# Raw tiles of p_v from four to eight, the order of products at the layer joints, and gates applied as scalars in a decoder trunk

## The chip, the cores and the metric

The kernel runs on one core of a Trainium2 chip, as one program. The metric is the device time of one execution in microseconds. Of the core's engines the text names TensorE (PE, with its weight loads as PEld), VectorE (DVE), ScalarE (ACT), GpSimd (POOL) and SyncE (SP), whose instruction stream here only issues DMA transfers.

## What is computed

Two layers over 256 positions of width 1024. Layer 0 is latent attention (MLA) and a PEER feed-forward layer, layer 1 is native sparse attention (NSA) and a second PEER. Each sub-layer ends in a normalization.

```python
x = layer_norm(ALPHA * x + f(x))          # after every sub-layer

def peer_ffn(x, w_q, subkeys, u, v):      # 16384 experts, 8 heads x 16 per token
    q = (xc @ w_q).reshape(PEER_CHUNK, PEER_HEADS, 2, PEER_DK // 2)
    ...                                   # top 16 x 16 of two key halves, best 16
    u_e = u[experts]
    v_e = v[experts]
    a = gelu(einsum("thkd,td->thk", u_e, xc))
    return einsum("thk,thkd->td", g * a, v_e)

def masked_softmax(sc, mask):             # NSA: one for each branch and head
    sc = jnp.where(mask, sc, NEG_INF)
    m = jnp.max(sc, axis=-1, keepdims=True)
    e = jnp.exp(sc - m) * mask
    return e / jnp.maximum(jnp.sum(e, axis=-1, keepdims=True), TINY)
...                                       # o = sum over 3 branches of gate[branch, head] * p @ v
```

## The kernel before

**Weights in two parts.** Every weight matrix is read from HBM as float32 tiles of 128x1024 (512 KB). A tile lands in a raw buffer. ScalarE casts it to a high part `hi` (L98), VectorE subtracts that from the raw tile and gets the low part `lo` (L109). Activations are split likewise, so a product needs up to three matmuls: high by high, high by low, low by high. All 603 tiles stand in one list, `self.stream`, in the order of use. `_sdma` requests them through SP's queue, `_shi` casts, `_slo` subtracts, and `nxt` hands out the next tile. There are four raw buffers. When `_slo` has recorded the subtraction of a tile, its raw buffer is free, and `_slo` requests the tile three places after the next one to be subtracted (`self.sl + self.nraw - 1`).

**Four parts of the program.** MLA lasts to about 124 us, then the first PEER, NSA, and the second PEER. A PEER layer reads 16 tiles of `p_wq` to route, then 128 tiles of `p_u` (the u phase, in which all activations of all experts are computed and those not chosen are masked), then 128 tiles of `p_v` (the v phase). A stretch between two parts, with sum, normalization, transposition and the first products of the next part, is called a joint here: joint 1 from MLA to the first PEER (about 113 to 132 us), joint 2 from there to NSA (868 to 890), joint 3 from NSA to the second PEER (1040 to 1061), and the end.

**The v phase.** For each tile j of `p_v` TensorE does ten matmuls of 128x512 (L160, in `v_mm`): six for the first 128 tokens (`tt` 0) and four for the second 128 (`tt` 1). Their other operand, `W`, is the masked activations of these 128 experts, split into parts on ScalarE (L740) and VectorE (L745). Of the second 128 tokens only 64 go through these matmuls, with high and low part of W side by side as 128 columns; so the result has the low part's product in its rows 64 to 127, and `sum_1` adds both halves (L812 to L814). The other 64 tokens have 128 experts each, and their rows of `p_v` are gathered: 64 indirect DMAs from GpSimd's queue (L447, `g_row`), 512 KB each, into a ring of ten buffers `row` and `more`. VectorE multiplies each row by its factor and adds it up (L461, `g_mac`, into `gacc`), from tile 7 on, one row per 1.77 tiles. Before that small gathers (L451, `g_act`) fetch the activations for the factors. After the last row `g_sum` (L805, L806) adds `gacc` to the residual `hN`. The kept tiles, the last eight, have their matmuls for `tt` 1 done in the joint, so that TensorE has work while the first half is normalized.

**The joint.** `ln_sum`, `ln_stats`, `ln_mid` and `ln_scale` normalize halves of 512 columns (L232, L235, L239 to L251, L257) on VectorE. `ln_aside` does one half of `tt` 0 on ScalarE (L266) and GpSimd (L267, L268). `ln_T` transposes on TensorE (L189) and splits into high part (L282, ScalarE) and low part (L283, VectorE) of the transposed activations `hT`. Low parts of the next weight tiles are made on GpSimd in that time (`self._slo(..., nc.gpsimd)`). `early_open` starts the next part's products with two tiles for `tt` 0, all three kinds, and `early_close` does the rest tile by tile.

**NSA.** Per pair of heads the scores come from TensorE, VectorE takes maxima and reciprocals and multiplies the probabilities `p` by them and by the gates (L1505 to L1526); for heads 8 to 13 a part of that runs on GpSimd. GpSimd also subtracts for the low part of q (L1323, `qs`) and zeroes three buffers (`hb`, `kcp` at L1375, `hidR` at L1384).

**What sets the order.** Instructions run on each engine in the order in which the code records them; a queue of DMA requests goes in order too. Most of the order is written out by hand, with deferred steps (`tick`, `run_side`) between them.

Of the kernel before, what the change touches and what calls it, by code (L numbers as in the profile page):

```python
# [37 lines left out]
RING, MORE, LEAD = 6, 4, 7  # L38
# [4 lines left out]
class Kern:  # L43
# [5 lines left out]
    def plan(self):  # L49
        I, L = self.I, []  # L50
        if "mla" in self.parts:
            L += [I["a_w_in"][k] for k in range(KC)]
            L += [I["a_wk"][i] for i in range(2)]
            L += [I["a_wq"][i] for i in range(3)]
            L += [I["a_wv"][i] for i in range(2)]
            L += [I["a_wq"][i] for i in range(3, 6)]
            L += [I["a_wo"][i] for i in range(KC)]
        for l in (0, 1):
# [8 lines left out]
            if f"peer{l}" in self.parts:  # L67
                L += [I["p_wq"][l, i] for i in range(16)]
                L += [I["p_u"][l, (P - FIRST + j) % P] for j in range(P)]
                L += [I["p_v"][l, j] for j in range(P)]  # L70
        self.stream = L
        self.si = 0
# [28 lines left out]
    def _slo(self, upto, eng=None):  # L101
        while self.sl <= min(upto, len(self.stream) - 1):
# [8 lines left out]
            self._sdma(self.sl + self.nraw - 1)  # L111
# [27 lines left out]
    def new_hT(self):  # L139

        self.hTT = self.pers.tile([P, KC, 2, S], F32R, tag="hT", name="hT")
# [119 lines left out]
    def ln_aside(self, tt, hf):  # L261

        nc, w = self.nc, self.lnw[tt]
        z, gb, acc = self.ln_half(tt, hf)
        nc.vector.scalar_tensor_tensor(w[:, 0:1], w[:, 2:3], -1.0, w[:, 7:8], op0=OP.mult, op1=OP.mult)
        nc.scalar.activation(z, z, AF.Identity, bias=w[:, 0:1], scale=w[:, 7:8])  # L266
        nc.gpsimd.tensor_tensor(z, z, gb[:, 0, :], op=OP.mult)  # L267
        nc.gpsimd.tensor_tensor(z, z, gb[:, 1, :], op=OP.add)  # L268
        if not self.want_T:
            nc.sync.dma_start(self.O[0, tt * P:(tt + 1) * P, hf * 512:(hf + 1) * 512], z)  # L270

# [13 lines left out]
    def ln_first(self):  # L285

        for hf in range(2):
            self.ln_sum(0, hf)
            self.ln_stats(0, hf)
        self.ln_mid(0)  # L290
        for hf in range(2):
            self.ln_scale(0, hf)
        lo = [self.ln_T(0, hf) for hf in range(2)]
        self.ln_sum(1, 0)
        lo[0]()
        self.ln_stats(1, 0)
        self.ln_sum(1, 1)
        lo[1]()
        self.ln_stats(1, 1)

    def ln_last(self, *los):
        los = list(los)
# [110 lines left out]
    def peer(self, l):  # L413
        tc, nc, I = self.tc, self.nc, self.I
        with ExitStack() as es:
# [23 lines left out]
            def g_row(c):  # L439
                if c >= P // 2:  # L440
                    return
                if c % (RING + MORE) >= RING:
                    t = more[:, c % (RING + MORE) - RING]
                else:
                    t = gat.tile([P, D], F32, tag="row", name="row", bufs=RING)
                grow[c] = t
                nc.gpsimd.indirect_dma_start(out=t, out_offset=None, in_=gtable,  # L447
                                             in_offset=bass.IndirectOffsetOnAxis(ap=gidx[:, 0, c:c + 1], axis=0))
# [5 lines left out]
            def g_mac(c):  # L454
# [7 lines left out]
                g_row(c + RING + MORE)  # L462
# [179 lines left out]
            if not hasattr(self, "eacc") or self.parts[0] == f"peer{l}":  # L642
                self._slo(self.si + 1)
# [140 lines left out]
            def v_mm(j, tt, blocks, start=False, stop=False):  # L784
# [8 lines left out]
            more = self.pers.tile([P, MORE, D], F32, tag="hT", name="more")  # L793
            rate, gc = (P - 8 - LEAD) / 64, 0

            fetch = deque([(g_row, c) for c in (RING, RING + 1)] + [(g_act, c) for c in range(4)] +
                          [(g_row, c) for c in (RING + 2, RING + 3)] + [(g_act, c) for c in range(4, 64)])
            summed = []

            def g_sum():  # L800

                t = gat.tile([P, D], F32, tag="row", name="gsum", bufs=RING)
                u, z = slice(P - GT, P), hN[P - GT:P, 1, :]
                nc.scalar.copy(t[u], gacc[0:GT])
                nc.vector.scalar_tensor_tensor(z, z, ALPHA, gacc[u], op0=OP.mult, op1=OP.add)  # L805
                nc.vector.tensor_tensor(z, z, t[u], op=OP.add)  # L806

            def sum_1(f):

                t = gat.tile([P, 512], F32, tag="row", name="low", bufs=RING)  # L810
                c, z = accs[1][f], hN[0:P - GT, 1, f * 512:(f + 1) * 512]
                nc.scalar.copy(t[0:P - GT], c[P - GT:P])  # L812
                nc.vector.scalar_tensor_tensor(z, z, ALPHA, c[0:P - GT], op0=OP.mult, op1=OP.add)
                nc.vector.tensor_tensor(z, z, t[0:P - GT], op=OP.add)  # L814

            for j in range(P):
# [14 lines left out]
                for _ in range(8 if j == 0 else 1):  # L831
                    if fetch:
                        f, c = fetch.popleft()
                        f(c)
# [3 lines left out]
                if gc == 64 and not summed:  # L838
                    summed.append(1)
                    g_sum()  # L840
# [12 lines left out]
            self.ln_scale(0, 0)  # L853
            if early:
                self._slo(self.si, nc.gpsimd)
            self.ln_aside(0, 1)
            for j in range(P - NT, P - 2):
# [776 lines left out]
```

## Time and profile before

| | us |
|---|---|
| median of three runs | 1817.84 (1814.76 to 1824.02) |
| the profiled execution | 1817.85 |
| its span in the trace | 1816.1 |
| VectorE, ScalarE, GpSimd busy | 1558.2, 1047.1, 490.7 |
| DMA over the span | 416.69 MB, 229 GB/s |

The clock that TensorE was granted is 0.987 of full speed over the span. The profile says for each group of instructions how long they ran, how long the engine sat idle before them, and whose event ended that idle time. Matmul ends are modelled; a matmul's start is measured. Distances between starts are therefore what is used for TensorE's pace.

### The profile page before, as it was taken

The numbers are of one execution on the slowest core, as the hardware profiler recorded it, in microseconds if no ns is written. First come the engines' busy times: TensorE is split into PE (matmuls) and PEld (weight loads), VectorE is DVE, ScalarE is ACT, GpSimd is POOL, SyncE is SP. The second block draws the span as 40 slices with busy tenths as digits, with TensorE's granted clock in tenths as the row PEclk, the third lists the DMA queues.
The fourth block names the chain that finished last, engine by engine and source line by source line (L and its number), as shares of the span: only waits on it lengthen the run. The fifth ranks groups of instructions, "written<-read, shape, count | busy, mean of one in ns | idle before, by whom it ended". The sixth has DMA issues, their size and how long they took to land. (4 is left out here: it accounts for less than half of the span.)

```text
span 1816.1 us, 30995 instructions
## 1 busy us (share of the span) xinstructions
PE 1747.9 (96%) x10610; PEld 1500.9 (83%) x10610; DVE 1558.2 (86%) x3692; ACT 1047.1 (58%) x2271; POOL 490.7 (27%) x457
## 2 busy tenths in 40 slices
PE   7989999999999999999898999999999999999996
PEld 6869999888888777887786689998888887778775
DVE  6778988889998889998658779988899986899998
ACT  6645456666666455555457645556666664555553
POOL 2120002000004776540533310011000016775510
PEclk9999999999999999999998999999999999999998
DMA  7545657555557999997661265656555558999983
GB/s 248 161 147 166 194 176 266 178 183 182 176 185 264 350 328 350 352 358 249 241 215 53 94 209 180 193 184 245 189 175 183 185 196 307 335 336 361 344 313 127
DMA packets 120653, 416.69 MB, mean 229 GB/s; under 512 B 18064, under 2 KB 20144, under 8 KB 119408
## 3 DMA queue, kind: packets, MB, share of 16 engines
q1 hardware_dynamic: 91008, 322.61, 53.0%
q0 software_dynamic: 29488, 92.10, 14.0%
q8 instruction: 84, 1.38, 0.3%
q14 instruction: 73, 0.60, 0.1%
HBM read 400.49 MB, written 13.63 MB: 228 GB/s over the span
## 5 line engine op out<-in xcount | busy, mean ns | idle before, releaser
L98 ACT CAST hi<-raw 128x1024 fp32r<-128x1024 f32 (+1 forms) x589 | 616.5, 1048 | 411.6 <-DMA raw<-p_v 140.6
L160 PE MATMUL mm<-hT,hi 128*128 128x256 f32 (+1 forms) x3360 | 845.9, 332 | 0.0
L109 DVE TENSOR_TENSOR lo<-raw,hi 128x1024 fp32r<-128x1024 f32 (+1 forms) x582 | 710.4, 1223 | 99.1 <-ACT hi L98 63.7
L160 PE MATMUL mm<-hT,lo 128*128 128x256 f32 x2376 | 639.7, 281 | 0.0
L160 PEld LDWEIGHTS mm<-hT,hi 128*128 128x128 f32 x3360 | 560.1, 190 | 48.0 <-issue 1.2
L160 PEld LDWEIGHTS mm<-hT,lo 128*128 128x128 f32 x2376 | 451.3, 190 | 13.4
L160 PE MATMUL acc<-hi,W 128*128 128x512 f32 x1476 | 420.9, 392 | 9.0 <-issue 5.0
L160 PEld LDWEIGHTS acc<-hi,W 128*128 128x128 f32 x1476 | 276.8, 188 | 73.5 <-issue 10.6
L160 PE MATMUL acc<-lo,W 128*128 128x512 f32 x984 | 310.7, 396 | 6.7 <-DVE lo L109 3.3
L729 POOL DMA_DIRECT2D actD<-gst x64 | 34.8, 544 | 799.1 <-ACT gst L727 799.1
L160 PEld LDWEIGHTS acc<-lo,W 128*128 128x128 f32 x984 | 181.6, 188 | 61.2 <-DVE lo L109 19.2
L451 POOL DMA_INDIRECT gel<-actD,gidx x128 | 149.7, 1170 | 39.0 <-issue 38.7
L447 POOL DMA_INDIRECT row<-p_v,gidx x80 | 118.1, 1476 | 111.1 <-DVE gacc L461 77.3
L721 ACT ACTIVATE mm<-mm 128x192 f32<-128x192 f32 (+23 forms) x170 | 40.9, 241 | 122.7 <-DVE mm L719 122.7
L745 DVE TENSOR_TENSOR W<-A,W 128x128 fp32r<-128x128 f32 (+1 forms) x512 | 108.1, 254 | 1.8 <-ACT W L740 1.8
L461 DVE SCALAR_TENSOR_TENSOR gacc<-row,gw,gacc 128x1024 f32<-128x1024 f32 x78 | 100.0, 1282 | 0.6
L740 ACT CAST W<-A 128x192 fp32r<-128x192 f32 x256 | 88.1, 346 | 0.0
L622 DVE SCALAR_TENSOR_TENSOR A<-acc,A 128x176 f32<-128x176 f32 (+16 forms) x268 | 56.2, 274 | 36.3 <-PE acc L160 34.0
L719 DVE TENSOR_TENSOR mm<-mm,half 128x256 f32<-128x256 f32 x174 | 74.8, 430 | 12.3 <-ACT half L718 11.7
L447 POOL DMA_INDIRECT more<-p_v,gidx x48 | 69.5, 1448 | 43.7 <-DVE gacc L461 34.3
L724 ACT ACTIVATE A<-mm 128x192 f32<-128x192 f32 (+23 forms) x244 | 67.7, 278 | 8.5 <-DVE lo L109 1.8
L718 ACT COPY half<-mm 128x256 f32<-128x256 f32 x174 | 66.0, 379 | 0.5 <-PE mm L160 0.5
(280 smaller groups left out, 1812.6 us busy)
## 6 DMA issues: line engine op xcount, KB each, us to landing
raw<-p_u SPq DMA_DIRECT2D x256, 512.0 KB
raw<-p_v SPq DMA_DIRECT2D x256, 512.0 KB
raw<-p_wq SPq DMA_DIRECT2D x32, 512.0 KB
actD<-gst POOLq DMA_DIRECT2D x64, 128.0 KB
raw<-b_wo SPq DMA_DIRECT2D x12, 512.0 KB
raw<-a_wo SPq DMA_DIRECT2D x8, 512.0 KB
raw<-s_wT SPq DMA_DIRECT2D x8, 512.0 KB
w<-c_w POOLq DMA_DIRECT2D x4, 1024.0 KB
```

The source lines that it names most:

```text
L98: self.nc.scalar.copy(self.his[i], self.raws[i])
L109: e.tensor_tensor(self.los[i], raw, self.his[i].bitcast(F32), op=OP.subtract)
L160: self.nc.tensor.matmul(out, a, b, start=start, stop=stop)
L447: nc.gpsimd.indirect_dma_start(out=t, out_offset=None, in_=gtable, in_offset=bass.IndirectOffsetOnAxis(ap=gidx[:, 0, c:c + 1], axis=0))
L451: nc.gpsimd.indirect_dma_start(out=gel[c // 4][:, c % 4:c % 4 + 1], out_offset=None, in_=gplaces, in_offset=bass.IndirectOffsetOnAxis(ap=g ...
L461: nc.vector.scalar_tensor_tensor(gacc, t, gw[:, c:c + 1], gacc, op0=OP.mult, op1=OP.add)
L622: nc.vector.scalar_tensor_tensor(y, pv[:, j0:j0 + m], 1.0 / GS, y, op0=OP.mult, op1=OP.mult)
L718: nc.scalar.copy(t, ps[:, S:2 * S])
L719: nc.vector.tensor_tensor(ps[:, 0:S], ps[:, 0:S], t, op=OP.add)
L724: nc.scalar.activation(y[:, n:ND], ps[:, n:ND], AF.Gelu)
L740: nc.scalar.copy(WW[j][:, 0:ND], slot(j))
L745: nc.vector.tensor_tensor(WW[j][:, o:o + c.stop - c.start], slot(j)[:, c], WW[j][:, c].bitcast(F32), op=OP.subtract)
```

## The change

Three groups of edits.

**The v phase.** The gather ring shrinks from ten buffers to six. The buffer of 2 MB that held the other four (`more`, in the place of `hT`, which is not needed during the v phase) becomes four more raw tiles (`spare`). `_ahead` says how far requests may run: in the v phase four tiles further than before, up to the next part's first four; shortly before the v phase not beyond its fourth tile. `g_sum` becomes three steps: `g_alpha` after row 60, `g_copy` after the last row, and a last addition one tile later.

**The joints.** `ln_aside` goes; VectorE normalizes all halves. The high parts of the next four tiles are cast early, and TensorE does all products with high parts (both parts of the activations) before any product with a low part. One low part is made on GpSimd, after a copy of one element that makes it wait for `ln_sum(1, 0)`; the others on VectorE, behind the normalization. The kept tiles are used in another order. `sum_1` reads the copied half from PSUM.

**Sparse attention.** The three buffers are zeroed at its start. q's low part moves to VectorE. The maximum with TINY goes (so the sum of exponentials is divided without that floor), and the gate becomes a second scalar of the multiplication.

```diff
-RING, MORE, LEAD = 6, 4, 7
+RING, LEAD = 6, 7
...
-            t = self.sraw.tile([P, n], F32, tag="raw", name="raw")
+            if self.spare is not None and self.v0 <= self.sd < self.v0 + P and (self.sd - self.v0) % 8 > 3:
+                t = self.spare[:, (self.sd - self.v0) % 8 - 4]
+            else:
+                t = self.sraw.tile([P, n], F32, tag="raw", name="raw")
...
-            self._sdma(self.sl + self.nraw - 1)
+            self._sdma(self._ahead())
+
+    def _ahead(self):
+        n, v0 = self.sl + self.nraw - 1, self.v0
+        if self.spare is not None:
+            n = max(n, min(n + 4, v0 + P + 3))
+        elif v0 - 4 < self.sl < v0 + P:
+            n = min(n, v0 + 3)
+        return n
...
+    def lo_aside(self):
+        t = self.small.tile([P, 1], F32, tag="aside", name="aside")
+        self.nc.gpsimd.tensor_copy(t, self.ln_half(1, 0)[0][:, 0:1])
+        self._slo(self.si, self.nc.gpsimd)
+
+    def ln_last(self, early):
+        los = []
+        if early:
+            self.early_open()
+            self.early_mm(0, 0, 0, (0, 1))
+            self.early_mm(0, 1, 0, (0, 1))
+        los.append(self.ln_T(0, 1))
+        if early:
+            self.early_mm(0, 0, 0, (2, 3))
         for hf in range(2):
             self.ln_scale(1, hf)
             los.append(self.ln_T(1, hf))
+            if early and hf == 0:
+                self.early_mm(1, 0, 0, (0, 1))
...
             def sum_1(f):
-                t = gat.tile([P, 512], F32, tag="row", name="low", bufs=RING)
+                t = self.ps()
                 c, z = accs[1][f], hN[0:P - GT, 1, f * 512:(f + 1) * 512]
+                nc.vector.scalar_tensor_tensor(z, z, ALPHA, c[0:P - GT], op0=OP.mult, op1=OP.add)
                 nc.scalar.copy(t[0:P - GT], c[P - GT:P])
-                nc.vector.scalar_tensor_tensor(z, z, ALPHA, c[0:P - GT], op0=OP.mult, op1=OP.add)
                 nc.vector.tensor_tensor(z, z, t[0:P - GT], op=OP.add)
...
     def early_close(self):
+        for tt in range(2):
+            for x in range(2):
+                self.early_mm(tt, x, 0, range(4))
         for q in range(4):
...
+            self._slo(self.ei + q)
+            if q > 1:
+                self._shi(self.ei + q + 2)
+            self.tick()
+            for tt in range(2):
+                self.early_mm(tt, 0, 1, (q,))
...
-                    nc.gpsimd.tensor_tensor(t[64:128, c], r[:, c], t[0:64, c].bitcast(F32), op=OP.subtract)
+                    nc.vector.tensor_tensor(t[64:128, c], r[:, c], t[0:64, c].bitcast(F32), op=OP.subtract)
...
-                    nc.vector.tensor_scalar(m[:, 2, :], m[:, 2, :], TINY, None, op0=OP.max)
                     nc.vector.reciprocal(m[:, 3, :], m[:, 2, :])
-                    gv = gates[:, :, 16:48].rearrange("p t (b h) -> p t b h", b=2)[:, :, :, h]
-                    nc.vector.tensor_tensor(m[:, 3, :].rearrange("p (t b) -> p t b", t=2),
-                                            m[:, 3, :].rearrange("p (t b) -> p t b", t=2), gv, op=OP.mult)
                     for br, eng in ((1, nc.gpsimd if 8 <= h < NH - 2 else nc.vector), (0, nc.vector)):
-                        eng.tensor_scalar(p[:, br, 0:P], p[:, br, 0:P], m[:, 3, br:br + 1], None, op0=OP.mult)
-                        eng.tensor_scalar(p[:, br, P:384], p[:, br, P:384], m[:, 3, 2 + br:3 + br], None, op0=OP.mult)
+                        for tt, c in enumerate((slice(0, P), slice(P, 384))):
+                            eng.tensor_scalar(p[:, br, c], p[:, br, c], m[:, 3, 2 * tt + br:2 * tt + br + 1],
+                                              gates[:, tt, 16 * br + 16 + h:16 * br + 17 + h], op0=OP.mult, op1=OP.mult)
```

How the order of instructions changes, at three places. Line numbers of the changed kernel are its own: L92 there is the request of a raw tile (L86 before), L181 the matmul (L160), L210 the transposition (L189), L115 the low part (L109).

SP's queue from the last tiles of the first u phase to NSA, before:

```order
L86 DMA raw<-p_wq 128x1024 x16
L86 DMA raw<-p_u 128x1024 x128
L86 DMA raw<-p_v 128x1024 x128
L86 DMA raw<-s_wv 128x1024 x4
L86 DMA raw<-s_wT 128x1024 x4
```

And now, its beginning:

```order
L92 DMA raw<-p_wq 128x1024 x16
L92 DMA raw<-p_u 128x1024 x128
L92 DMA raw<-p_v 128x1024 x4
L92 DMA spare<-p_v 128x1024 x4
L92 DMA raw<-p_v 128x1024 x4
L92 DMA spare<-p_v 128x1024 x4
```

The same 128 transfers stand in the same order; every second four of them go to other buffers, so that a request waits for the tile eight places earlier instead of four.

TensorE in joint 2, from the last products with W (`keep` are the kept tiles; `hi,hT` and `lo,hT` are the first products of NSA, with a weight's high or low part; `ident,hN` are transpositions), before:

```order
L160 MATMUL acc<-lo,W 128x512
L189 MATMUL mm<-ident,hN 128x128 x4
L160 MATMUL acc<-hi,hT 128x512 x8
L160 MATMUL acc<-lo,hT 128x512 x4
L189 MATMUL mm<-ident,hN 128x128 x8
L160 MATMUL acc<-hi,hT 128x512 x4
L160 MATMUL acc<-lo,hT 128x512 x2
L160 MATMUL acc<-hi,hT 128x512 x4
L160 MATMUL acc<-lo,hT 128x512 x2
```

And now:

```order
L181 MATMUL acc<-keep,W 128x512 x16
L210 MATMUL mm<-ident,hN 128x128 x4
L181 MATMUL acc<-keep,W 128x512 x4
L181 MATMUL acc<-hi,hT 128x512 x8
L210 MATMUL mm<-ident,hN 128x128 x4
L181 MATMUL acc<-hi,hT 128x512 x4
L210 MATMUL mm<-ident,hN 128x128 x4
L181 MATMUL acc<-hi,hT 128x512 x4
L210 MATMUL mm<-ident,hN 128x128 x4
L181 MATMUL acc<-hi,hT 128x512 x16
L181 MATMUL acc<-lo,hT 128x512 x16
```

Products with high parts now stand between the transpositions, and all sixteen products with low parts at the end; after the last transposition there are 32 products instead of 36.

VectorE in NSA at the first head's probabilities (`m` holds maxima, sums and reciprocals, `qs` q's parts), before:

```order
L1507 TENSOR_SCALAR m<-m 128x4
L1396 TENSOR_TENSOR vcp<-mm,m_10029 128x512 x2
L1505 TENSOR_REDUCE m<-mm 128x2
L1506 TENSOR_REDUCE m<-acc 128x2
L1507 TENSOR_SCALAR m<-m 128x4
L1519 TENSOR_SCALAR m<-m 128x4
L1520 RECIPROCAL m<-m 128x4
L1522 TENSOR_TENSOR m<-m,gates 128x4
L1525 TENSOR_SCALAR p<-p,m 128x128
```

And now:

```order
L1508 TENSOR_SCALAR m<-m 128x4
L1330 TENSOR_TENSOR qs<-qr,qs 64x512 x2
L1397 TENSOR_TENSOR vcp<-mm,m_9993 128x512 x2
L1506 TENSOR_REDUCE m<-mm 128x2
L1507 TENSOR_REDUCE m<-acc 128x2
L1508 TENSOR_SCALAR m<-m 128x4
L1521 RECIPROCAL m<-m 128x4
L1524 TENSOR_SCALAR p<-p,m,gates 128x128
```

Two small operations are gone from each head's chain, and in four places of VectorE's order two subtractions for q stand ahead of reductions.

More of the change, by code (lines that the diff above doesn't have):

```diff
@@ L110, in _slo, with more_raw @@
             self.sl += 1
-            self._sdma(self.sl + self.nraw - 1)
+            self._sdma(self._ahead())
[6 more added lines that the diff above has]
+        return n
+    def more_raw(self):
+        self.spare = self.pers.tile([P, 4, D], F32, tag="hT", name="spare")
+        self._sdma(self._ahead())
     def nxt(self, prep=True, tick=True):
@@ L439, in g_row @@
             def g_row(c):
[L440 to L448, printed above, removed]
+                if c < P // 2:
+                    t = grow[c] = gat.tile([P, D], F32, tag="row", name="row", bufs=RING)
+                    nc.gpsimd.indirect_dma_start(out=t, out_offset=None, in_=gtable,
+                                                 in_offset=bass.IndirectOffsetOnAxis(ap=gidx[:, 0, c:c + 1], axis=0))
             def g_act(c):
@@ L791, in v_mm, with g_alpha, g_copy @@
                         self.mm(accs[tt][f], xx, ww[:, f * 512:(f + 1) * 512], go, end)
-            more = self.pers.tile([P, MORE, D], F32, tag="hT", name="more")
             rate, gc = (P - 8 - LEAD) / 64, 0
[L796 to L800, printed above, removed]
+            self.more_raw()
+            gu, late_sums = slice(P - GT, P), deque()
+            def g_alpha():
+                nc.vector.scalar_tensor_tensor(gacc[gu], hN[gu, 1, :], ALPHA, gacc[gu], op0=OP.mult, op1=OP.add)
+            def g_copy():
                 t = gat.tile([P, D], F32, tag="row", name="gsum", bufs=RING)
[L803 to L806, printed above, removed]
+                nc.scalar.copy(t[gu], gacc[0:GT])
+                late_sums.append(lambda: nc.vector.tensor_tensor(hN[gu, 1, :], gacc[gu], t[gu], op=OP.add))
             def sum_1(f):
-                t = gat.tile([P, 512], F32, tag="row", name="low", bufs=RING)
+                t = self.ps()
                 c, z = accs[1][f], hN[0:P - GT, 1, f * 512:(f + 1) * 512]
+                nc.vector.scalar_tensor_tensor(z, z, ALPHA, c[0:P - GT], op0=OP.mult, op1=OP.add)
                 nc.scalar.copy(t[0:P - GT], c[P - GT:P])
-                nc.vector.scalar_tensor_tensor(z, z, ALPHA, c[0:P - GT], op0=OP.mult, op1=OP.add)
                 nc.vector.tensor_tensor(z, z, t[0:P - GT], op=OP.add)
@@ L830, in peer @@
                 kept[j] = (hi, lo, WW.pop(j))
[L831 to L834, printed above, removed]
+                for c in range(4) if j == 0 else range(j + 3, min(j + 4, 64)):
+                    g_act(c)
+                if late_sums:
+                    late_sums.popleft()()
                 while gc < 64 and j >= LEAD + int(rate * gc):
@@ L837, in peer @@
                     gc += 1
-                if gc == 64 and not summed:
-                    summed.append(1)
-                    g_sum()
+                    if gc in (60, 64):
+                        late_sums.append((g_alpha, g_copy)[gc == 64])
                 v_mm(j, 0, (0, 1), j == 0, j == P - 1)
@@ L1129, in out_close @@
             self.ln_stats(0, hf)
-        for k in ([5] if again else range(KC - self.kept + 1, 6)):
-            self.out_mm(k, 1, two, False, False)
+        if again:
+            self.out_mm(5, 1, two, False, False)
         if again:
@@ L1260, in nsa @@
             pcT = mp.tile([P, 2, S], F32, name="pcT")
+            hb = tmp.tile([P, 256], F32, tag="hb", name="hb", bufs=1)
+            hr = tmp.tile([P, 2, G, HG, 16], F32, tag="hidR", name="hidR", bufs=1)
+            for x in (hb, kcp, hr):
+                nc.gpsimd.memset(x, 0.0)
             if "peer0" not in self.parts:
-                self._slo(self.si + 1)
+                self._shi(self.si + 3)
                 self.early_open()
```

134 lines of the change are left out of this document (48 added, 86 removed).

## The prediction

> **What bounds the kernel now.** I read the page first, then the table of windows, then waits and single rows.
>
> ```profile
> PE 1747.9 (96%) x10610; PEld 1500.9 (83%) x10610; DVE 1558.2 (86%) x3692; ACT 1047.1 (58%) x2271; POOL 490.7 (27%) x457
> ...
> L109 DVE TENSOR_TENSOR lo<-raw,hi 128x1024 fp32r<-128x1024 f32 (+1 forms) x582 | 710.4, 1223 | 99.1 <-ACT hi L98 63.7
> ```
>
> TensorE is busy for 96% of the span, so nothing here shortens work; only its gaps can go. The windows say where they lie. The columns are the window, its length, then PE, weight loads, DVE, ACT and POOL, the granted clock, the DMA share and GB/s.
>
> ```profile
> 300.00:400.00 100.00, 100.00 (x677) 87.48 (x676) 86.69 (x217) 66.29 (x187) 5.76 (x10) 1.00 0.61 208
> 561.90:870.30 308.40, 300.41 (x1285) 239.22 (x1283) 275.63 (x476) 167.22 (x260) 170.02 (x128) 0.99 0.90 324
> 1489.50:1803.00 313.50, 302.30 (x1280) 238.46 (x1279) 276.08 (x476) 166.13 (x259) 160.79 (x127) 0.99 0.87 311
> 885.00:1042.00 157.00, 144.25 (x1005) 117.73 (x1003) 111.84 (x245) 98.58 (x243) 59.38 (x65) 0.96 0.47 157
> ```
>
> A u phase (first row) has no gap, and the change leaves it alone. The two v phases (rows 2 and 3, from the first product with W to the last) and the sparse attention (row 4) have them. "Busy" hides part of it, because each matmul's modelled duration overlaps the next one's start. The pace shows it better:
>
> ```profile
> 862.76 4.70 PE L160 MATMUL acc<-keep,W 128*128 128x512 f32 x20
> 867.29 0.61 PE L160 MATMUL acc<-hi,W 128*128 128x512 f32 x2
> ```
>
> Twenty products start in 867.29 − 862.76 = 4.53 us, 0.2265 us each. A v phase has 128 tiles × 10 products, 1280 × 0.2265 = 289.9 us. So the phases lose 308.4 − 289.9 = 18.5 and 313.5 − 289.9 = 23.6 us, **42 us** together. What ends the gaps:
>
> ```profile
> ACT hi L98 <- DMA raw<-p_v: 140.6, 109, 5.0
> ```
> ```profile
> 1507.03 0.33 SPq L86 DMA_DIRECT2D raw<-p_v  x1
> ```
> ```profile
> 1523.03 1.04 ACT L98 CAST hi<-raw 128x1024 fp32r<-128x1024 f32 x1 [6.51 <-PE acc L160]
> ```
> ```profile
> 1728.73 6.63 DMA raw<-p_v
> ...
> 1743.15 8.58 DMA raw<-p_v
> ...
> 1786.05 5.16 DMA raw<-p_v
> ```
>
> ScalarE waits 109 times for a raw tile of p_v. One was requested at 1507.03 and only cast at 1523.03, 16 us later; the releaser that this row names had long been done. On the chain of waits single raw transfers take 5.2 to 8.6 us. Four raw tiles at 10 × 0.2265 = 2.27 us of TensorE each give a request at most 9.1 us. So in the v phases late raw tiles are the limit, and not mainly the rate of the DMA:
>
> ```profile
> 700.00:750.00 50.00, 49.63 (x217) 40.04 (x216) 47.94 (x82) 28.85 (x46) 30.06 (x20) 1.00 0.98 357
> ...
> 1700.00:1750.00 50.00, 49.51 (x213) 39.25 (x212) 46.33 (x79) 27.14 (x42) 20.07 (x12) 1.00 0.95 352
> ```
>
> With 357 GB/s moving, 217 products start in 50 us, 0.2304 each, nearly full pace.
>
> **Part A, eight raw tiles in the v phase.** Four rows of the gather ring become four raw tiles: a raw request gets 8 × 2.27 = 18.1 us instead of 9.1, above the 16 us seen. No work is added on an engine, and SP's queue holds the same transfers. What stays of the 42: the DMA rate, and gaps whose releaser is not a raw tile. For the first I take the 0.2304 as pace where rows and raws both flow (113 tiles, since macs start at tile 7 and end at 120): 113 × 10 × 0.0039 = 4.4 us a layer, 9 in all. At the 0.2347 of 1700 to 1750 it would be 9.3 a layer, 19 in all. For the second, 11 us, half of it in the restart of layer 1:
>
> ```profile
> 1519.45 0.39 PE L160 MATMUL acc<-hi,W 128*128 128x512 f32 x1 [1.13 <-DVE gacc L461]
> 1520.87 0.39 PE L160 MATMUL acc<-hi,W 128*128 128x512 f32 x1 [1.03 <-issue]
> ```
>
> Here the next product starts 1.4 us after the one before, and for 1.03 of them TensorE waits for nothing that the trace shows. So 20 of 42 stay, and A gives **−22**; bounds −33 (only 9 stay) and 0 (all of it is rate). VectorE doesn't hinder that: it is busy 275.63 us of the first v phase, over 128 tiles 2.15 us a tile, under TensorE's 2.27, though close. The split g_sum is in the 42: two 64x1024 operations in a row hold up a low part, and TensorE.
>
> ```profile
> 847.98 1.22 DVE L805 SCALAR_TENSOR_TENSOR hN<-hN,gacc 64x1024 f32<-64x1024 f32 x1
> 849.31 1.22 DVE L806 TENSOR_TENSOR hN<-hN,gsum 64x1024 f32<-64x1024 f32 x1
> ```
>
> **Part B, the joints.** A GpSimd operation holds up VectorE. Joint 1:
>
> ```profile
> 116.35 1.82 DVE L239 SCALAR_TENSOR_TENSOR hN<-hN,lnw,gb 128x512 f32<-128x512 f32 x1
> 118.08 0.15 DVE L248 RECIPROCAL lnw<-lnw 128x1 f32<-128x1 f32 x1
> 118.27 2.11 DVE L249 SCALAR_TENSOR_TENSOR lnw<-lnw 128x1 f32<-128x1 f32 x1
> ```
> ```profile
> 115.21 5.16 POOL L109 TENSOR_TENSOR lo<-raw,hi 128x1024 fp32r<-128x1024 f32 x2
> ```
> ```profile
> 120.42 0.73 PE L160 MATMUL acc<-lo,hT 128*128 128x512 f32 x2 [2.02 <-POOL lo L109]
> ```
>
> Joint 2 without a GpSimd operation beside it:
>
> ```profile
> 876.25 0.74 DVE L239 SCALAR_TENSOR_TENSOR hN<-hN,lnw,gb 128x512 f32<-128x512 f32 x1
> 876.90 0.15 DVE L248 RECIPROCAL lnw<-lnw 128x1 f32<-128x1 f32 x1
> 877.10 0.22 DVE L249 SCALAR_TENSOR_TENSOR lnw<-lnw 128x1 f32<-128x1 f32 x1
> ```
>
> And joint 3:
>
> ```profile
> 1045.20 2.11 DVE L249 SCALAR_TENSOR_TENSOR lnw<-lnw 128x1 f32<-128x1 f32 x1
> ```
>
> Joint 1 loses (1.82 − 0.74) + (2.11 − 0.22) = 3.0 us, joint 3 at least 2.11 − 0.22 = 1.9, and TensorE waits with them. After the change one low part of 2.6 us (half of 5.16) runs on GpSimd, released after the first half's sum; it should end about when L239 starts, so I credit 2 us in each. The copy that gates it waits for VectorE's sum; behind it on GpSimd's queue stand only loads for the next stage, which before stood behind two low parts. After the last transposition 32 products are left instead of 36, 4 × 0.227 = 0.9. Joints 1 and 3: −2.9 each. Joint 2 and the end, the sum of the last 64 tokens:
>
> ```profile
> 870.97 0.68 DVE L813 SCALAR_TENSOR_TENSOR hN<-hN,acc 64x512 f32<-64x512 f32 x1 [2.86 <-ACT low L812]
> ```
> ```profile
> 1803.35 0.68 DVE L813 SCALAR_TENSOR_TENSOR hN<-hN,acc 64x512 f32<-64x512 f32 x1 [1.81 <-ACT low L812]
> 1804.06 1.58 DVE L814 TENSOR_TENSOR hN<-hN,low 64x512 f32<-64x512 f32 x1
> ```
>
> The first operation no longer waits for ScalarE's copy (I take 1.5 us of joint 2's 2.86 and 0.7 of the end's 1.81; the rest is the wait for the products that are summed), and L814 returns from 1.58 to 0.68. The copy now goes to PSUM; L813 reads PSUM already and takes the same 0.68 as I expect of L814. Joint 2: −1.5 − 0.9, and about 0.9 from products that need no low part yet, −3.3. The end has no such products: −0.7 − 0.9, so −1.6. The half of the normalization that VectorE takes over (L239 and L257 once more, 0.74 each) lies beside the kept products, 32 × 0.227 = 7.3 us; uncovered it would cost 1.5 in each of four places. Low parts are late next: three of 1.22 on VectorE after the last hT, needed one per 0.9 us (four products), behind sixteen products with high parts; they just fit. B: **−11**, bounds −14 and −4.
>
> **Part C, sparse attention.** Over 16 heads a chain loses two small operations, and GpSimd's subtraction of q moves to VectorE.
>
> ```profile
> L1323 POOL TENSOR_TENSOR qs<-qr,qs 64x512 fp32r<-64x512 f32 x8 | 10.2, 1292 | 11.8 <-issue 8.6 <-ACT qs L1322 3.1
> ```
> ```profile
> L1522 DVE TENSOR_TENSOR m<-m,gates 128x4 f32<-128x4 f32 x16 | 4.4, 274 | 0.6
> ...
> L1519 DVE TENSOR_SCALAR m<-m 128x4 f32<-128x4 f32 x16 | 2.6, 163 | 0.0
> ...
> L1378 DVE TENSOR_TENSOR kcp<-mm,m 128x240 f32<-128x240 f32 x2 | 0.7, 403 | 2.2 <-POOL kcp L1375 2.2
> ```
>
> Removed on VectorE: 4.4 + 2.6 = 7.0 us, and a wait of 2.2 for kcp's zeroing, which now runs long before. Added: eight subtractions of 64x512, about 0.7 each (L813 has that width), 5.6. Only some of the chain shows on TensorE, since the in-order queue now also waits for ScalarE's cast before each subtraction. I take **−3**, bounds −6 and +3.
>
> By the Trainium skill ("SBUF — State Buffer", section "Who interferes with whom") a VectorE operation with two inputs in SBUF blocks against a GpSimd operation that reads SBUF, for its whole length. The joint rows agree: 118.27 + 2.11 = 120.38 is when GpSimd's 115.21 + 5.16 ends. The moved subtraction has two such inputs, so by that rule it can be blocked in its turn; that is the third rival.
>
> **Sum.** −22 − 11 − 3 = −36 against the profiled execution of 1817.85 (span 1816.1, 1.7 around it; the median of the runs is 1817.84): **1782 us**.
>
> **Rivals.**
> 1. *The DMA rate is the limit.* Deeper requests move no more bytes. For it: shares of 0.95 to 0.98 in both rows above. Against: 0.90 and 0.87 over whole phases. Then A is between 0 and −8: 1817.85 − 4 − 14 = about 1800. Chance 0.17.
> 2. *The gather ring runs dry (slower).* Six rows instead of ten: a row freed by one mac is used six macs later, 6 × 1.77 × 2.3 = 24.4 us. The layer's last row, and its mac:
>
> ```profile
> 806.29 3.49 POOL L447 DMA_INDIRECT row<-p_v,gidx  x1 [2.47 <-DVE gacc L461]
> ```
> ```profile
> 846.66 1.29 DVE L461 SCALAR_TENSOR_TENSOR gacc<-row,gw,gacc 128x1024 f32<-128x1024 f32 x1
> ```
> ```profile
> 1706.61 5.79 DMA row<-p_v,gidx
> ```
> ```profile
> q0 software_dynamic: 2060, 6.56, 36.2%
> ```
>
> Ten macs left it 846.66 − 809.78 = 37 us from issue to use. If landing takes over 20 us beside eight raw requests, VectorE stalls in order, the low parts behind it too. Rows are used at one per 1.77 × 2.3 = 4.1 us. If they land at one per 4.8, then after some 10 us of slack 0.7 × 58 rows − 10 = 31 us a layer go, 62 in all: 1782 + 62 = 1844. It turns slower from 4.6 on (2 × (0.48 × 58 − 10) = 36). Against it stands the row on the chain that took 5.8 us, far below 20. For it: in 700 to 750 the software queue, which carries the rows, moved no more than was used, 6.56 MB, a row of 0.52 MB per 4.0 us. Chance 0.07.
>
> The Trainium skill ("DMA: Bandwidth & Descriptors", section "Queues, rings and completion order") says that a DMA engine takes turns between queues by packets. By that the gather would get up to half of 357 GB/s, a row per 2.9 us, and this rival could not occur; the 36.2% of that stretch is no even share, so I leave it a chance.
>
> 3. *The sparse attention gives back.* Eight subtractions each wait as long as they take, 0.7, for a GpSimd operation or for ScalarE's cast, and the scores behind them in VectorE's queue wait too: 5.6 us, C is about +3, the time 1788. Chance 0.12.
> 4. *The requests don't run ahead,* because freeing a raw tile stays tied to the low part, which is made late: A gives −2 or −3 and the joints −4, 1811. Chance 0.06.
>
> **How the numbers follow.** The forecast has 0.58. Its own range, 1765 to 1798, comes from A's −33 and −8; rivals 1 and 3 widen it to **1765 to 1806**. A measurement of this kernel can tell about 0.5%, 9 us, from no change. Faster by over that: forecast, rival 3 and most of rival 1, 0.84. Within: rival 4 and the rest, 0.09. Slower: rival 2, 0.07.
>
> **What would show it.** A: p_v's line in the waits falls from 140.6 to under 60 us, and the v windows to about 297 and 300 us. B: L239 and L249 at 0.74 and 0.22 in joints 1 and 3. C: the window of the sparse attention 3 us shorter. I am wrong if VectorE waits for a row, or if the v windows stay above 305 us with the DMA share at 0.95.

## The result and the profile after

| | changed | before |
|---|---|---|
| median of four runs each, one chip (us) | 1792.29 (1791.22 to 1795.45) | 1818.10 (1814.76 to 1824.02) |
| profiled execution, its span | 1791.22, 1789.4 | 1817.85, 1816.1 |

The changed kernel is faster by 25.8 us, ratio 0.9849 [0.9816, 0.9883]. The prediction was 1782 (1765 to 1806): the sign and the range are right, 10 of the 36 us are missing. The page of the changed kernel, span and busy times:

```profile
span 1789.4 us, 30937 instructions
...
PE 1730.8 (97%) x10610; PEld 1489.2 (83%) x10610; DVE 1554.7 (87%) x3675; ACT 1042.2 (58%) x2267; POOL 494.5 (28%) x441
```

TensorE starts the same 10610 matmuls, so the spans can be compared mark by mark: the first transposition of a joint, the first product of the next part (`mm<-hT`), the first and the last product with W.

| stretch | before | after | difference | predicted |
|---|---|---|---|---|
| up to the first transposition of joint 1 | 111.8 | 111.2 | -0.6 | |
| joint 1 | 21.4 | 17.4 | -4.1 | -2.9 |
| routing and u phase, layer 0 | 428.6 | 428.2 | -0.4 | 0 |
| v phase, layer 0 | 308.4 | 300.1 | -8.3 | -22 in both |
| joint 2, from the last product with W | 20.1 | 20.5 | +0.4 | -3.3 |
| NSA | 149.6 | 145.9 | -3.7 | -3 |
| joint 3 | 20.9 | 16.4 | -4.5 | -2.9 |
| routing and u phase, layer 1 | 428.6 | 428.6 | 0 | 0 |
| v phase, layer 1 | 313.7 | 309.0 | -4.7 | |
| from the last product with W to the end | 12.9 | 12.2 | -0.7 | -1.6 |

The differences add up to -26.6; the spans differ by 26.7, and the rest is rounding. The two v phases gave 13 of the 22 us forecast for them. They are in the table of windows, with the columns that the prediction explains (the second window ends just before the last product starts). The forecast had named 297 and 300 us for them:

```profile
556.80:856.90 300.10, 295.65 (x1284) 239.00 (x1283) 276.43 (x478) 168.23 (x262) 180.94 (x126) 1.00 0.91 333
1468.30:1777.10 308.80, 299.80 (x1280) 239.74 (x1279) 276.54 (x478) 164.25 (x257) 176.51 (x126) 0.99 0.88 318
```

The waits that end idle time, with us in total, times, and the longest:

```profile
ACT hi L104 <- PE acc L181: 189.0, 158, 5.9
POOL row L453 <- DVE gacc L467: 90.7, 60, 4.5
ACT hi L104 <- DMA spare<-p_v: 5.4, 6, 1.6
```

Of the 140.6 us of waits for raw tiles of p_v, 5.4 are left, all for the four new buffers (`spare`); the forecast said "under 60". ScalarE now waits for TensorE, up to 5.9 us at a time. To see where the v phases still lose, each is cut at tile 62 of 128. The loss of a stretch is the time between the starts of its first and last product, less 0.227 us a product:

```
loss in us       layer 0: tiles 0-31  31-62  62-120  rest   layer 1: 0-31  31-62  62-120  rest
before                    4.4   4.5   4.7   4.4               8.3   6.4   4.5   4.2
changed                   0.0   9.6  -0.2   0.4               7.9  11.0  -0.2   0.0
```

Behind tile 62 the losses went from 17.8 to 0.0 us. In the first 62 tiles they went from 23.6 to 28.5. So the change removed the loss behind tile 62 completely and did not lessen the other. ScalarE at the worst place, with the releaser in brackets:

```profile
1592.12 1.05 ACT L104 CAST hi<-spare 128x1024 fp32r<-128x1024 f32 x1 [3.49 <-PE acc L181]
...
1599.34 1.05 ACT L104 CAST hi<-spare 128x1024 fp32r<-128x1024 f32 x1 [5.92 <-PE acc L181]
...
1606.47 1.05 ACT L104 CAST hi<-spare 128x1024 fp32r<-128x1024 f32 x1 [5.83 <-PE acc L181]
```

There are four `hi` buffers, so a cast waits for the products of the tile four places earlier. By the count of products the cast of 1606.47 (tile 54) waited for a product of tile 50 whose modelled end is 1594.09: the permission came 12.4 us after that end. Its raw tile had been requested at 1581.9. TensorE falls behind in the same stretch. Its first product of tile 53 starts 0.30 us after that tile's cast (1599.34) has ended, as if it had waited for it, but the profile names no releaser:

```profile
1600.69 0.73 PE L181 MATMUL acc<-hi,W 128*128 128x512 f32 x2 [0.75 <-issue]
```

What GpSimd does meanwhile:

```profile
1600.82 0.95 POOL L457 DMA_INDIRECT gel<-actD,gidx  x1 [0.30 <-issue]
1602.08 1.03 POOL L457 DMA_INDIRECT gel<-actD,gidx  x1 [0.30 <-issue]
...
1605.14 0.95 POOL L457 DMA_INDIRECT gel<-actD,gidx  x1 [0.30 <-issue]
```

These are the small gathers of `g_act` (128 values of 4 bytes each, one gather a tile and four more at the start), and they run until tile 60. That made them the suspect.

### The profile page after: what moved, and what is told of

It is laid out like the page before. It is cut to its first block, busy times and chain, and to the rows that moved or that the text cites. A ratio compares the mean times of both kernels' runs of the same rounds, so it can differ in the third digit from the quotient of the medians.

```text
span 1789.4 us, 30937 instructions
## 1 busy us (share of the span) xinstructions
PE 1730.8 (97%) x10610; PEld 1489.2 (83%) x10610; DVE 1554.7 (87%) x3675; ACT 1042.2 (58%) x2267; POOL 494.5 (28%) x441
## 3 DMA queue, kind: packets, MB, share of 16 engines
q0 software_dynamic: 29488, 92.10, 13.9%
## 5 line engine op out<-in xcount | busy, mean ns | idle before, releaser
L181 PE MATMUL mm<-hT,hi 128*128 128x256 f32 (+1 forms) x3360 | 838.6, 330 | 0.0
L181 PE MATMUL mm<-hT,lo 128*128 128x256 f32 x2376 | 638.2, 281 | 1.1 <-DVE lo L115 1.0
L104 ACT CAST hi<-raw 128x1024 fp32r<-128x1024 f32 (+1 forms) x463 | 484.2, 1048 | 255.2 <-PE acc L181 87.3
L115 DVE TENSOR_TENSOR lo<-raw,hi 128x1024 fp32r<-128x1024 f32 (+1 forms) x459 | 559.1, 1221 | 44.0 <-ACT hi L104 32.6
L181 PEld LDWEIGHTS mm<-hT,hi 128*128 128x128 f32 x3360 | 552.2, 188 | 49.3 <-issue 1.2
L181 PEld LDWEIGHTS mm<-hT,lo 128*128 128x128 f32 x2376 | 448.3, 189 | 15.5 <-DVE lo L115 1.9
L181 PE MATMUL acc<-hi,W 128*128 128x512 f32 x1476 | 419.6, 392 | 6.3 <-issue 4.7
L181 PEld LDWEIGHTS acc<-hi,W 128*128 128x128 f32 x1476 | 276.8, 188 | 71.5 <-issue 11.7
L181 PE MATMUL acc<-lo,W 128*128 128x512 f32 x984 | 307.3, 393 | 7.1 <-issue 4.7
L453 POOL DMA_INDIRECT row<-p_v,gidx x128 | 220.8, 1725 | 132.8 <-DVE gacc L467 90.7
L181 PEld LDWEIGHTS acc<-lo,W 128*128 128x128 f32 x984 | 183.3, 188 | 54.8 <-issue 10.2
L104 ACT CAST hi<-spare 128x1024 fp32r<-128x1024 f32 x126 | 132.3, 1050 | 139.9 <-PE acc L181 101.7
L115 DVE TENSOR_TENSOR lo<-spare,hi 128x1024 fp32r<-128x1024 f32 x126 | 153.7, 1220 | 26.7 <-issue 16.9
L467 DVE SCALAR_TENSOR_TENSOR gacc<-row,gw,gacc 128x1024 f32<-128x1024 f32 x126 | 161.3, 1280 | 1.1
L725 DVE TENSOR_TENSOR mm<-mm,half 128x256 f32<-128x256 f32 x174 | 74.4, 428 | 15.1 <-ACT half L724 14.7
```

The costliest lines, as they stand in the source:

```text
L104: self.nc.scalar.copy(self.his[i], self.raws[i])
L115: e.tensor_tensor(self.los[i], raw, self.his[i].bitcast(F32), op=OP.subtract)
L181: self.nc.tensor.matmul(out, a, b, start=start, stop=stop)
L467: nc.vector.scalar_tensor_tensor(gacc, t, gw[:, c:c + 1], gacc, op0=OP.mult, op1=OP.add)
L725: nc.vector.tensor_tensor(ps[:, 0:S], ps[:, 0:S], t, op=OP.add)
```

## The experiments

Twelve runs, on five chips, named B to F. "Before" is the kernel before on the same chip; its time was 1795 to 1797 us on four of them and 1813 us on one (B), which itself became part of the answer. Which chip the pair above ran on is not known; it is called A here, and A and B may be the same chip.

**The parts alone (chip C).** Three kernels each keep one part of the diff shown with the change and have the rest as before: the v phase (`only_v`), the joints with sparse attention (`joints_nsa`), the sparse attention alone (`only_nsa`). A fourth is the changed kernel with four raw tiles:

```diff
     def _ahead(self):
         n, v0 = self.sl + self.nraw - 1, self.v0
-        if self.spare is not None:
-            n = max(n, min(n + 4, v0 + P + 3))
-        elif v0 - 4 < self.sl < v0 + P:
-            n = min(n, v0 + 3)
         return n
...
-            self.more_raw()
```

> The kernel before with the edits of the v phase alone (eight raw tiles, gather ring of six, g_sum in three steps). By the prediction's sum it is 22 us under the kernel before, about 1796. By the trace of the changed kernel, where the two v windows lost 8.3 and 4.7 us, it is 13 under it, about 1805.

> The kernel before with the edits of the joints and of the sparse attention, without those of the v phase. By the prediction's sum 11 + 3 = 14 us under the kernel before, about 1804; if the v phase brought 13 of the 26 us measured, 13 under it, about 1805. If the parts help or hinder each other, the gains of this run and of the one with the v phase alone don't add up to 26.

> The kernel before with the edits of the sparse attention alone. By the prediction 3 us faster, about 1815; by its third rival 3 us slower, about 1821.

> The changed kernel with four raw tiles in the v phase as before; the gather ring of six, the split g_sum, the joints and the sparse attention stay changed. If late raw tiles cost what the prediction said, the 18 to 22 us that it gave to them come back: about 1810 to 1814. If most of what is lost in a v phase lies in its first 61 tiles, where the raw tiles of the changed kernel land in time and TensorE waits nevertheless, only the losses of the later tiles come back, some 8 us in all: about 1800.

Before took 1796.09 us on this chip.

| | us | ratio | difference |
|---|---|---|---|
| only_v | 1777.07 | 0.9891 [0.9868, 0.9913] | -19.0 |
| joints_nsa | 1786.76 | 0.9946 [0.9928, 0.9963] | -9.3 |
| only_nsa | 1793.09 | 0.9991 [0.9974, 1.0009] | -3.0, not to be told from 0 |
| raws4 | 1780.98 | 0.9909 [0.9885, 0.9933] | -15.1 |

```
loss in us       layer 0: tiles 0-31  31-62  62-120  rest   layer 1: 0-31  31-62  62-120  rest
only_nsa (v phase of before)   0.0   0.6   4.9   4.9         -0.1   1.4   1.6   4.1
only_v                         0.5  -0.1  -0.2   0.4          0.5  -0.1  -0.2   0.0
raws4                         -0.1   0.6   3.7   2.7         -0.1  -0.1   4.8   3.7
```

On this chip the first 62 tiles lose next to nothing, whatever the kernel, and that is why before is some 20 us faster here than on chip A. Behind tile 62 the picture is that of chip A: 15.5 us lost with four raw tiles and the old ring, 14.9 with four raw tiles and the rest of the change, 0.0 with eight. Against the 1768 us to which the two parts add up (19.0 + 9.3 off 1796.1), four raw tiles cost 13 us, between the 8 and the 18 to 22 that were expected. The raw tiles are late in those stretches; the waits of `raws4`:

```profile
ACT hi L104 <- DMA raw<-p_v: 176.7, 136, 4.0
```

**Again, and without the small gathers (chip B).** The second kernel leaves out the 64 small gathers of each layer; the factors are made from ones instead of the gathered activations.

```diff
-                for c in range(4) if j == 0 else range(j + 3, min(j + 4, 64)):
-                    g_act(c)
+                if j == 0:
+                    for x in gel:
+                        nc.gpsimd.memset(x, 1.0)
```

> The changed kernel once more, to stand beside parts of it on one chip. On the chip of the four runs before, the v phase's edits alone brought 19.0 us and the other two groups 9.3; if they add up, the changed kernel is 28 us under the kernel before where that takes about 1796, so about 1768. If the chip is like that of the first pair (kernel before about 1818), it takes about 1792 again, with the first 62 tiles of each v phase 9 and 19 us over 620 products at 0.227 us.

> The changed kernel without the 64 small gathers (128 elements of 4 bytes each) of activations in each v phase; their target is filled with ones instead, so the sum over the last 64 tokens is another one. If these gathers are what holds up the first 62 tiles on the chip of the first pair, those tiles take their 141 us there and the time falls by 28 us, to about 1764; where the first 62 tiles lose nothing already, nothing changes (within 3 us of the changed kernel). If the large gathers or the reload of hN hold them up, it stays at about 1790 on a chip like the first.

Before took 1813.19 us here, the changed kernel 1795.61 (0.9884 [0.9831, 0.9938]), and without small gathers 1764.54 (0.9719 [0.9667, 0.9771]). The changed kernel lost 32.3 us in the first 62 tiles of both layers, the other one at most 0.4 us in any of the eight stretches. Its v phases, and ScalarE in the second:

```profile
558.20:848.60 290.40, 290.40 (x1285) 240.50 (x1283) 277.79 (x478) 169.69 (x262) 109.45 (x78) 1.00 0.92 344
1460.50:1750.40 289.90, 289.90 (x1281) 240.11 (x1279) 277.64 (x478) 165.80 (x257) 111.19 (x78) 1.00 0.90 339
```
```profile
1578.10 1.05 ACT L104 CAST hi<-spare 128x1024 fp32r<-128x1024 f32 x1 [0.97 <-PE acc L181]
...
1580.36 1.06 ACT L104 CAST hi<-raw 128x1024 fp32r<-128x1024 f32 x1 [0.96 <-PE acc L181]
```

The windows are the 289.9 us of full pace, and every cast waits 0.96 us for TensorE, as it must when TensorE sets the pace. How much later than the modelled end of the freeing product a cast starts, counted from tile 4 on:

```
us late, mean and most       layer 0: before tile 62   after it     layer 1: before tile 62   after it
changed kernel, chip A            2.39   9.0      0.04   0.0         2.71  12.4      0.06   1.1
changed kernel, chip B            2.68   9.7      0.05   0.8         2.17  10.4      0.59   7.7
no small gathers, chip B          0.14   1.8      0.04   0.0         0.09   1.8      0.04   0.0
only_v, chip C                    0.12   1.9      0.04   0.0         0.08   1.8      0.04   0.0
```

The 7.7 on chip B belongs to a stall that began at tile 60 and ended 2 us after the last small gather. So on chips A and B casts start late beside the small gathers; on chip B leaving the gathers out ends it. On chip C the same gathers at the same rate do no harm.

**Other rates and shapes of the small gathers (chip D).** `slow_tiny` issues eight at the start and then 0.565 a tile, `fast_tiny` two a tile, and `wide16` fetches 16 values instead of one, at the slow rate, and picks the right one on VectorE with a mask.

```diff
-                for c in range(4) if j == 0 else range(j + 3, min(j + 4, 64)):
+                na = lambda j: min(64, 8 + int(0.565 * j)) if j >= 0 else 0
+                for c in range(na(j - 1), na(j)):
```
```diff
-                for c in range(4) if j == 0 else range(j + 3, min(j + 4, 64)):
+                for c in range(4) if j == 0 else range(2 * j + 2, min(2 * j + 4, 64)):
```
```diff
-                nc.gpsimd.indirect_dma_start(out=gel[c // 4][:, c % 4:c % 4 + 1], out_offset=None, in_=gplaces,
...
+                nc.gpsimd.indirect_dma_start(out=gel[c // 4][:, c % 4], out_offset=None, in_=gplaces,
...
+                    nc.vector.tensor_tensor(e, e, mask[:, None, :].to_broadcast([P, 4, 16]), op=OP.mult)
+                    nc.vector.tensor_reduce(gw[:, c:c + 4], e, axis=AX.X, op=OP.add)
```

> The changed kernel with the 64 small gathers of a v phase spread over 100 tiles (eight at the start, then 0.565 a tile) instead of 61. On a chip where the kernel before takes about 1815: if each small gather costs a fixed delay, the loss of some 28 to 32 us stays and only moves to later tiles, about 1793; if it is a matter of how many are under way at once, it falls, to 1780 or less. On a chip where the kernel before takes about 1796 nothing changes against about 1768.

> The changed kernel with two small gathers a tile, done after 31 tiles. On a chip like the first: fixed delay for each, about 1793 with the loss in the first 31 tiles and none behind; if density matters, more than 1793. On a chip where they cost nothing, about 1768.

> The changed kernel with each small gather fetching 64 bytes per partition instead of 4, at the slow rate; VectorE picks the element with a mask (two more small operations per four gathers, some 6 us of VectorE in a layer). If the size of 4 bytes is what matters, the loss goes on a chip like the first: about 1768 to 1772; if the number of descriptors matters (128 for each gather, as before), it stays with slow_tiny.

Before took 1796.52 us, as on chip C, so this is no chip like A. `slow_tiny` took 1765.53 (0.9828 [0.9809, 0.9848]), `wide16` 1772.28 (0.9865 [0.9848, 0.9881]; its two added operations take 13.9 us of VectorE in all), `fast_tiny` 1823.60 (1.0153 [1.0137, 1.0170]). `fast_tiny` lost 27 and 30 us in the first 62 tiles, but for another reason. VectorE waits for gathered rows:

```profile
DVE gacc L467 <- DMA row<-p_v,gidx: 58.9, 21, 5.4
```

A small gather holds GpSimd for about 0.95 + 0.30 us (the rows above). Two a tile, 2.5 us, are more than a tile's 2.27, so the row gathers behind them in the queue are issued late and the ring runs dry. That is a full GpSimd queue, and no evidence on the late casts. These three runs settle nothing about the late casts.

**Two more chips (E and F).** `slow_tiny_2` and `slow_tiny_3` repeat `slow_tiny`; `raws4_no_tiny` has four raw tiles and no small gathers.

> The changed kernel with its 64 small gathers spread over 100 tiles, once more, for a chip like the first (kernel before about 1815). There: a fixed delay for each small gather would leave it at about 1793 with losses up to tile 100; if they cost only when they follow each other closely, about 1766. On a chip where the kernel before takes about 1796, about 1766 again.

> The changed kernel with four raw tiles and without the small gathers (the sum over the last 64 tokens is another one). What four raw tiles lose by themselves then shows, whatever the chip: 15 us over the two v phases by the run with four raw tiles, so about 1780, with the losses behind tile 62, where the gathers of rows keep the DMA full. If the small gathers were behind those losses too, about 1765.

> The changed kernel with its 64 small gathers spread over 100 tiles, a third time, for a chip like the first (kernel before about 1815). There: about 1793 if each small gather costs a fixed delay, about 1766 if they cost only when they follow each other closely. On a chip where the kernel before takes about 1796, about 1766 again.

On chip E before took 1796.67, `slow_tiny_2` 1765.43 (0.9843 [0.9817, 0.9868]) and `raws4_no_tiny` 1781.46 (0.9927 [0.9905, 0.9948]); on chip F before took 1795.13 and `slow_tiny_3` 1760.18 (0.9813 [0.9792, 0.9834]). By before's time neither is a chip like A. The waits of `raws4_no_tiny`:

```profile
ACT hi L104 <- DMA raw<-p_v: 145.7, 118, 4.2
```

With four raw tiles the raws are late with or without small gathers, and the 16.0 us between the two kernels of chip E (the intervals do not overlap) are the raw tiles' worth; they differ in the small gathers too, but beside those `slow_tiny_2` keeps the full pace, with at most 0.5 us lost in any stretch. `slow_tiny` is the fastest version timed that computes everything. The changed kernel was not timed on chips D to F; the parts on chip C would put it at 1768 there, so spreading the gathers is worth little where casts are not late. Whether it cures them on a chip like A was not tried: it ran on none.

## Why the prediction was right, and where it was not

**Part A, the term that was mis-sized.** The step "so in the v phases late raw tiles are the limit" held for 17.8 of the 42 us, all of them behind tile 62, and there every one went; `raws4` and `only_v`, which lose 14.9 and 0.0 us there on one chip, show that it was the raw tiles. What the forecast let stay was 20: 9 for the DMA rate and 11 for gaps with another releaser. The first measured 0. Here are the first 62 tiles without small gathers on chip B:

```profile
558.20:698.70 140.50, 140.50 (x621) 116.37 (x620) 133.83 (x230) 81.75 (x128) 62.51 (x50) 1.00 0.98 370
```

At a DMA share of 0.98 and 370 GB/s, TensorE is at full pace: a high share was taken for a limit, and the pace of 0.2304 beside it had another cause. The second term was not 11 but 28.5, the loss of the first 62 tiles, where casts start late. The 16 us of the raw tile cast at 1523.03, on which the forecast rested, lie in that stretch. Its row named TensorE as releaser, and I set that aside because TensorE "had long been done": by the count of products its buffer came free at 1511.9, 11 us before the cast. In the rows of after it is just such a permission from TensorE that comes late, so that row was no evidence for a late raw tile. A takes the loss from 41 to 29 us, -13 and not -22; on chip C, with no late casts, A alone is -19.0.

**Part B, right in mechanism.** VectorE in joint 1, GpSimd's low part, and VectorE in joint 3:

```profile
116.07 0.74 DVE L260 SCALAR_TENSOR_TENSOR hN<-hN,lnw,gb 128x512 f32<-128x512 f32 x1
...
116.93 0.22 DVE L270 SCALAR_TENSOR_TENSOR lnw<-lnw 128x1 f32<-128x1 f32 x1
```
```profile
113.30 2.39 POOL L115 TENSOR_TENSOR lo<-raw,hi 128x1024 fp32r<-128x1024 f32 x1
```
```profile
1027.20 0.74 DVE L260 SCALAR_TENSOR_TENSOR hN<-hN,lnw,gb 128x512 f32<-128x512 f32 x1
...
1028.05 0.22 DVE L270 SCALAR_TENSOR_TENSOR lnw<-lnw 128x1 f32<-128x1 f32 x1
```

Both operations take the 0.74 and 0.22 that were forecast, and GpSimd is done at 113.30 + 2.39 = 115.69, before the first starts. By the Trainium skill ("SBUF — State Buffer", section "Who interferes with whom") they could block each other only while both run, and with them apart in time nothing is blocked; the rows agree. The sizes have a second cause, the granted clock. Joints 1, 2 and 3 and NSA of before, then the three joints of after, as windows (PE busy is the second number behind the window, the clock the third from the end):

```profile
111.80:133.30 21.50, 16.63 (x72) 12.69 (x72) 16.64 (x22) 8.84 (x12) 12.54 (x13) 0.92 0.56 180
869.10:890.40 21.30, 16.18 (x70) 12.21 (x69) 15.13 (x24) 8.53 (x12) 12.01 (x15) 0.92 0.48 153
1040.00:1060.90 20.90, 17.77 (x71) 13.43 (x70) 16.06 (x22) 7.73 (x11) 12.10 (x13) 0.84 0.60 198
890.40:1040.00 149.60, 136.88 (x972) 111.95 (x971) 108.06 (x240) 96.09 (x240) 55.12 (x60) 0.95 0.46 153
```
```profile
111.20:128.60 17.40, 15.43 (x71) 11.52 (x71) 14.70 (x24) 5.08 (x8) 7.38 (x11) 1.00 0.51 170
855.80:877.40 21.60, 17.83 (x70) 13.10 (x69) 15.21 (x25) 5.78 (x10) 10.57 (x17) 0.84 0.51 168
1023.30:1039.70 16.40, 14.95 (x71) 11.66 (x70) 13.52 (x22) 4.46 (x7) 7.46 (x11) 1.00 0.54 166
```

In joint 1 TensorE's idle time fell from 21.50 - 16.63 = 4.9 to 2.0, the forecast 2.9; another 1.2 came from nearly the same number of products at full clock. In joint 3 idle fell by 1.7 and busy by 2.8. In joint 2 idle fell too, by 1.4, but the clock dropped to 0.84 and took 1.7 back. The same joint in `slow_tiny`:

```profile
847.40:866.50 19.10, 15.12 (x70) 11.16 (x69) 15.19 (x25) 4.81 (x8) 8.94 (x14) 1.00 0.47 139
```

At full clock it takes 2.5 us less than in the pair's profile, 2.2 less than before, of which 1.1 is idle time; forecast was 3.3. All three profiles with the old joints show a dip in joints 1 and 3, and none of those with the new joints does; in joint 2 the new code dips in some executions and not in others, after the same gap. Here is that gap in the pair's profile, where the clock is 0.50 for the 6.8 us from 864.0 on, and in `slow_tiny`, where it stays at 1.00:

```profile
863.25 1.45 PE L181 MATMUL acc<-hi,hT 128*128 128x512 f32 x4 [2.16 <-ACT hT L292]
```
```profile
854.86 1.20 PE L181 MATMUL acc<-hi,hT 128*128 128x512 f32 x4 [2.16 <-ACT hT L292]
```

The longest gap of TensorE in a joint of before is 2.0 us (joints 1 and 3) or 2.8 us (joint 2), and in each of the three the clock dips; in the new joints 1 and 3 it is 0.7 us. So the shorter gaps and the full clock go together. The Trainium skill ("TensorE: Matmul & The Clock Gate", section "Part 1: The HAM clock gate (the "warmup" mystery)") lets the clock fall after an idle window of about 3.4 us that runs freely. A window that runs freely fits the same gap dipping only sometimes, but these dips come after gaps of 2.0 to 2.8 us, shorter than the 3.4; no run here shows the windows. The sum of the last 64 tokens no longer waits as long, and its second operation is short, as forecast, but waits for a copy in its turn:

```profile
1778.17 0.68 DVE L818 TENSOR_TENSOR hN<-hN,mm 64x512 f32<-64x512 f32 x1 [0.62 <-ACT mm L817]
```

So the end gained 0.7 instead of 1.6: the forecast had this wait, 0.62 us in each half of the sum, at nothing. For joint 2 it also took 0.9 us off the second operation, from the 1.58 of the end's row 1804.06. In joint 2 that operation was short before, in both halves:

```profile
871.69 0.68 DVE L814 TENSOR_TENSOR hN<-hN,low 64x512 f32<-64x512 f32 x1
...
874.31 0.86 DVE L814 TENSOR_TENSOR hN<-hN,low 64x512 f32<-64x512 f32 x1
```

Of the 11 us forecast for B the pair gave about 9. Some 6.7 of them are the mechanism (idle time in the three joints, and the end); the other 2 are the clock, which the forecast did not have, and that is luck. The joints with sparse attention measured -9.3 on chip C against -14 forecast.

**Part C, not measurable.** NSA became 3.7 us shorter in the pair, about as forecast, and I do not credit it: with the new code it took 145.9 us on chip A and 151.8 on chip E, before 149.6. The two extremes differ in the clock:

```profile
877.40:1023.30 145.90, 132.43 (x971) 107.91 (x970) 108.87 (x218) 97.15 (x243) 43.92 (x48) 0.98 0.47 158
```
```profile
875.60:1027.40 151.80, 138.78 (x972) 112.78 (x971) 108.09 (x218) 98.42 (x243) 42.18 (x51) 0.92 0.47 158
```

In the pair TensorE's idle time in NSA did not even fall: 149.60 - 136.88 = 12.7 us before, 145.90 - 132.43 = 13.5 after. What became shorter is busy time, at a clock of 0.98 instead of 0.95. Alone the change of this part has the ratio 0.9991 [0.9974, 1.0009].

**The rivals.** The DMA rate (1) is refuted by the 370 GB/s at full pace. The ring that runs dry (2) did not occur in the changed kernel, where VectorE never waits for a row; `fast_tiny` shows that such a stall is real and makes the kernel slower, but it came from GpSimd's queue and not from six buffers. The sparse attention giving back (3) can't be told from the clock's scatter; of its condition the trace shows that the eight subtractions take 0.69 us each (median), that VectorE waits 4.3 us in all for ScalarE's casts before them, and that TensorE waits for one of them, 1.3 us. That the requests do not run ahead (4) is refuted by p_v's waits, 5.4 us instead of 140.6.

**What stays open.** Why casts start up to 12 us late beside 4-byte gathers, and why only on some chips. The runs show that it goes with the small gathers on one chip and that it is not the raw tiles; they do not tell the transfers from GpSimd's work of issuing them. The path on which the permission is held up is narrowed by the trace's record of signals. In the first 62 tiles of layer 1, TensorE's products give 124 signals in which others can see that they are done. In the changed kernel on chip A 96 are recorded, and 52 of them within 0.06 us of their product's modelled end; without small gathers on chip B it is 124 and 123, on chip C (`only_v`) the same. The cast of 1606.47 starts 0.03 us after a recorded signal. So ScalarE goes on at once, and it is TensorE's signal that is recorded late. VectorE's signals are incomplete there too (129 of 225, those within 0.08 us of an operation's end), so that some may merely be missing from the record; what holds them up is not shown. TensorE itself also waits there without a releaser, up to 1.0 us a time:

```profile
1605.03 1.44 PE L181 MATMUL acc<-hi,W 128*128 128x512 f32 x3 [1.00 <-issue]
```

## What to carry to other kernels

Cut a lossy phase into stretches before putting one cause on it: here less than half of the loss went with more raw tiles, and the rest, on chip B, with the small gathers. Where a row names a releaser that "had long been done", work out both when the data landed and when the buffer was free, instead of passing the blame to the DMA; and a DMA share of 0.98 is no limit until the pace shows it. When a part's stretch is compared between two executions, read the granted clock of that stretch first, since a dip of a few us can hide or double a small gain.

## What the runs showed of the hardware that was not expected

On chips A and B (perhaps one chip) a waiting engine went on late, by up to 12.4 us, while GpSimd issued gathers of 4 bytes a partition; the first 62 tiles of both layers lost 28.5 and 32.3 us there, and before is 17 to 23 us slower on A and B than on the other four. The granted clock fell to half for 3.4 or 6.8 us after gaps of TensorE of 2.0 to 2.8 us, and after the same gap of 2.16 us in one execution and not in another. DMA sustained 370 GB/s for 140 us beside TensorE at full pace. A wait between two VectorE operations, for a copy of ScalarE that starts only after the first one, cost 0.62 us each of the four times.
